# Tree attention on one core: all work in groups of eight heads, stores of eight heads after the loads, V copies shared out anew, the first K and Q in fp32

## The chip, the cores and the metric

The kernel runs on one core of one Trainium2 chip. The metric is the device time of one execution in microseconds (us); lower is better. Times of the kernel before come from three runs; the profile is of one further execution.

## The reference

Attention over 96 independent heads (8 x 12) of 512 positions with 64 values each. A query may look at itself and at its ancestors in a binary tree whose node i has the parent (i - 1) // 2, so at ten keys at most. Inputs and output are fp32.

```
scores = np.einsum('bhqd,bhkd->bhqk', Q, K) * scale
scores = scores + (1 - mask) * (-1e9)
weights = np.exp(scores - np.max(scores, axis=-1, keepdims=True))
weights = weights / (np.sum(weights, axis=-1, keepdims=True) + 1e-10)
return np.einsum('bhqk,bhkd->bhqd', weights, V).astype(np.float32)
```

## The kernel before

**Work.** The 96 heads are taken two at a time: 48 pairs, and one pass of the main loop for each. A partition p holds the four nodes 4p to 4p+3 of a head. For pair i TensorE (PE) transposes K and Q into the PSUM tile `kqp` (L233), VectorE (DVE) copies that to the bf16 tile `kq` (`evac`, L259), PE makes the scores in two PSUM tiles (`scores1`, L270 and L275, and `scores2`, L293 and L299; the mask is a product of code vectors added to the scores), ScalarE (ACT) takes the exponentials (L281, L304), PE multiplies with V (`values`, L328) into the PSUM tile `ob`, and DVE divides by the row sums (`norm`, L351 and L352) into the output tile `of`. The PSUM pools for scores, transposes and products have one buffer each.

**V has to be laid out anew.** Loaded V (`vst`) is copied into one of two tiles `vt` of sixteen heads each, with the column of ones already in it. Three helpers do it, all recorded at L198: `spread_top` copies 32 partitions to one of four places (four copies), `spread_l7` copies two slots of 32 partitions (four copies), and `spread_leaves` two slots of 64 partitions (two copies). Before the change a group of V is sixteen heads. DVE makes nearly all of top and l7 and one of the two leaf copies, ACT makes the other leaf copies, and GpSimd (POOL) makes only the top copies of heads 0 to 7.

**Loads and stores.** K, Q and V are cast from fp32 to bf16 by the DMA, and all of these loads are issued by POOL (`load`, L185). K and Q tiles hold eight heads, in four buffers each; V tiles hold sixteen, in three. A store (`store`, L360) writes four heads, 512 KB, from one of 14 tiles `of`; POOL issues 23 of them, SP and ACT the last four heads. Everything POOL does lies in one list, `pool_program`, and after each pass `pool(i)` issues from its head as long as the next entry is `ready`. Loads and stores alternate in it from the load of heads 48 on. The main loop of a pass is: scores1(i), scores2(i), values(i-1), norm(i-1), transpose(i+2) and evac(i+2), spread(i), pool(i).

**Waits that the code does not name.** The framework adds a semaphore wait wherever an instruction depends on another engine's. The DMAs of POOL use eight semaphores in turn, so a DMA of POOL also waits until the DMA eight places before it in POOL's list has landed. POOL works its list in order: what stands behind a waiting entry waits too.

**At the start** the constants come by two queues: `ptile` (permutations) by SP, `ctile` (mask codes) by ACT; then POOL loads K and Q of two heads, V of four heads, and so on. PE runs products of zeros (`fill`) meanwhile.

Of the kernel before, what the change touches and what calls it, by code (L numbers as in the profile page):

```python
# [98 lines left out]
def kernel(  # L99
# [13 lines left out]
    NQ = NH // 4  # L113
    NP = 2 * NQ
    KB, VB = 8, 16
    assert NH % VB == 0
# [19 lines left out]
    vloads = ctx.enter_context(tc.tile_pool(name="vloads", bufs=3))  # L136
# [3 lines left out]
    opool = ctx.enter_context(tc.tile_pool(name="opool", bufs=14))  # L140
# [3 lines left out]

    ptile = consts.tile([P, perm_np.shape[1]], bf16)
    nc.sync.dma_start(out=ptile[:, :], in_=perm_dram.ap())
    ctile = consts.tile([P, code_np.shape[1]], bf16)
    nc.scalar.dma_start(out=ctile[0:BITS, :], in_=code_dram.ap())
# [21 lines left out]
    for n in range(NV):  # L170
        vt_n = consts.tile([P, VB, 5, D + 2], bf16, name=f"vt{n}")
        nc.vector.memset(vt_n[:, :, :, D:D + 1], 1.0)
        vts.append(vt_n)

    nc.vector.tensor_copy(out=ctile[64:64 + BITS, :], in_=ctile[0:BITS, :])
# [4 lines left out]
    def load(kept, pool, name, size, src, h0, n):  # L180

        b = h0 // size
        if h0 % size == 0:
            kept[b] = pool.tile([P, size, 4, D], bf16, name=name)
        nc.gpsimd.dma_start(  # L185
            out=kept[b][:, h0 % size:h0 % size + n, :, :].rearrange("p h t d -> p h (t d)"),
            in_=src[:, h0:h0 + n, :],
        )

    def load_qk(h0, n):  # L190
        load(ksts, loads, "kst", KB, Kr, h0, n)
        load(qsts, loads, "qst", KB, Qr, h0, n)

    def load_v(h0, n):
        load(vsts, vloads, "vst", VB, Vr, h0, n)

    def copy(eng, out, in_):
        (eng.copy if eng is nc.scalar else eng.tensor_copy)(out=out, in_=in_)  # L198

    def spread_top(eng, j, o, h0, h1):  # L200
        copy(
            eng, vts[o % NV][32 * j:32 * j + 32, h0:h1, 0, 0:D],
            vsts[o][0:32, h0:h1, UNITS[TOP + j][1], :],
        )

    def spread_leaves(eng, r, o, h0, h1):

        p = 64 if r else 0
        copy(
            eng, vts[o % NV][p:p + 64, h0:h1, 1 + r:4 + r:2, 0:D],  # L210
            vsts[o][64:128, h0:h1, r:3 + r:2, :],
        )

    def spread_l7(eng, quad, o, h0, h1):

        first, slot, step = ((2, 0, 3), (2, 2, -1), (1, 3, -3), (1, 1, 1))[quad]
        src = vsts[o][32:64, h0:h1, slot, :]
        src = bass.AP(
            src.tensor, src.offset, [list(src.ap[0]), list(src.ap[1]), [step * D, 2], [1, D]]
        )  # L220
        copy(eng, vts[o % NV][32 * quad:32 * quad + 32, h0:h1, first:first + 3:2, 0:D], src)

    def transpose_one(dst, i, a, t, units, st, perm):

        step = units[1] - units[0]
        if units[2] - units[1] == step:
            dst = dst[64 * a:64 * a + 64, units[0]:units[3] + 1:step, :]
        else:
            gap = units[2] - units[0]
            dst = dst[64 * a:64 * a + 64, units[0]:units[0] + 2 * gap, :].rearrange(  # L230
                "p (x y) c -> p x y c", x=2
            )[:, :, 0:2, :]
        nc.tensor.transpose(  # L233
            out=dst, in_=st[2 * i // KB][:, 2 * i % KB + a, t, :], identity=perm
        )
# [84 lines left out]
    def values(i):  # L320

        if i not in obs:
            obs[i] = psO.tile([P, 2, 512], fp32, name="ob")
        ob = obs[i]
        e1, e2, vt = ets[i], e2s[i % NE], vts[(2 * i // VB) % NV]

        def product(e, a, t, tile_v, lo=0, hi=128, **flags):
# [3 lines left out]
                rhs=vt[:, 2 * i % VB + a, tile_v, 0:D + 1],  # L331
# [3 lines left out]
        for a in range(2):  # L335
# [4 lines left out]
        for a in range(2):  # L340
# [4 lines left out]
    def norm(i):  # L345
        q, r = divmod(i, 2)
        if r == 0:
            ofs[q] = opool.tile([P, 4, 4, D], fp32, name="of")
        o4 = obs[i][:, :, 0:260].rearrange("p a (t c) -> p a t c", c=D + 1)
        rec = small.tile([P, 2, 4, 1], fp32, name="rec")  # L350
        nc.vector.reciprocal(out=rec[:, :, :, :], in_=o4[:, :, :, D:D + 1])  # L351
        nc.vector.tensor_tensor(  # L352
            out=ofs[q][:, 2 * r:2 * r + 2, :, :],
            in0=o4[:, :, :, 0:D],
            in1=rec[:, :, :, :].to_broadcast([P, 2, 4, D]),
            op=ALU.mult,
        )

    def store(eng, q, h0=0, n=4):
        eng.dma_start(  # L360
            out=Or[:, 4 * q + h0:4 * q + h0 + n, :],
            in_=ofs[q][:, h0:h0 + n, :, :].rearrange("p h t d -> p h (t d)"),
        )


    def pool_program():

        def tops(h0, h1):
            return [(spread_top, nc.gpsimd, j, 0, h0, h1) for j in range(4)]

        def stores(*qs):
            return [(store, nc.gpsimd, q) for q in qs]

        ops = [(load_qk, 0, 2), (load_v, 0, 4), (load_qk, 2, 2), (load_qk, 4, 4), (load_v, 4, 4)]
        ops += [(load_v, 8, 8), (load_qk, 8, 4)] + tops(0, 4) + [(load_qk, 12, 4)] + tops(4, 8)
        ops += [(load_qk, 16, 8), (load_v, 16, 8), (load_v, 24, 8), (load_qk, 24, 8)]
        ops += [(load_v, 32, 8), (load_v, 40, 8), (load_qk, 32, 8)]
        ops += [(load_v, 48, 8), (load_v, 56, 8), (load_qk, 40, 8)]
        for g, qs in ((6, (0,)), (7, (1,)), (8, (2, 3)), (9, (4, 5))):
            ops += [(load_v, 8 * g + 16, 8), (load_qk, 8 * g, 8)] + stores(*qs)  # L380
        ops += [(load_qk, 80, 4)] + stores(6, 7) + [(load_qk, 84, 4)] + stores(8, 9)
        ops += [(load_qk, 88, 4)] + stores(10, 11, 12) + [(load_qk, 92, 2)] + stores(13, 14)
        ops += [(load_qk, 94, 2)] + stores(*range(15, NQ - 1))
        return ops

    def ready(op, i):

        f, args = op[0], op[1:]
        if f is load_qk:
            return i >= 4 * (args[0] // KB) - 15  # L390
        if f is load_v:
            return i >= (-1, -1, -1, 3, 11, 15)[args[0] // VB]
        if f is spread_top:
            return True
        return 2 * i >= 4 * (args[1] + 1)

    def early(i):

        v, s = nc.vector, nc.scalar
        l7 = lambda ks, o, h0, h1: [(spread_l7, v, k, o, h0, h1) for k in ks]  # L400
        top = lambda ks, o, h0, h1: [(spread_top, v, k, o, h0, h1) for k in ks]
        leaf = lambda ks, o, h0, h1: [(spread_leaves, s, k, o, h0, h1) for k in ks]
        if i == 0:
            return l7(range(4), 0, 0, 4) + leaf((0, 1), 0, 0, 4)
        if i == 1:
            return l7(range(4), 0, 4, 8) + leaf((0, 1), 0, 4, 8)
        if i == 2:
            return top(range(4), 0, 8, 16)
        if i == 3:
            return l7(range(4), 0, 8, 16) + leaf((0, 1), 0, 8, 16)  # L410
        if i in (6, 7, 8):
            h = (0, 8)
        elif i in (9, 10, 11):
            h = (8, 16)
        else:
            return []
        n = i % 3
        return [top(range(3), 1, *h) + leaf((0,), 1, *h),
                top((3,), 1, *h) + l7((0, 1), 1, *h) + leaf((1,), 1, *h),
                l7((2, 3), 1, *h)][n]  # L420

    def spread(i):

        if i < 12:
            todo = early(i)
        else:
            v, s = nc.vector, nc.scalar
            o, k = divmod(i + 7, 8)
            if o < 2 or o >= NH // VB:
                todo = []  # L430
            else:
                top = [(spread_top, v, j) for j in range(4)]
                l7 = [(spread_l7, v, j) for j in range(4)]
                leaf = [(spread_leaves, v, 0)] + [(spread_leaves, s, 1, h, h + 8) for h in (0, 8)]
                todo = [top[:2], top[2:], leaf[:2], l7[:1], l7[1:2] + leaf[2:], l7[2:3], l7[3:], []]
                if o == 2:
                    todo = [[], [], [], top[:3], top[3:] + leaf[:2], l7[:2] + leaf[2:], l7[2:], []]
                todo = [op[:3] + (o,) + (op[3:] or (0, VB)) for op in todo[k]]
        for op in todo:
            op[0](*op[1:])  # L440

    program = pool_program()

    def pool(i):
        while program and ready(program[0], i):
            op = program.pop(0)
            op[0](*op[1:])

    AHEAD = {1: (2,), 2: (3,), 3: (4, 5)}

    pool(-1)
    fill(0, 9)
# [4 lines left out]
    fill(0, 8)  # L457
    transpose(1)
    fill(0, 4)
# [4 lines left out]
    for i in range(1, NP + 1):  # L464
# [3 lines left out]
        if i >= 2:  # L468
            values(i - 1)
            norm(i - 1)  # L470
# [6 lines left out]
        if i == NP - 1:  # L477
            store(nc.sync, NQ - 1, 0, 2)
    assert not program
    store(nc.sync, NQ - 1, 2, 1)  # L480
    store(nc.scalar, NQ - 1, 3, 1)

# [29 lines left out]
```

## Time and profile before

| | |
|---|---|
| median of three runs | 138.98 us (138.44 to 139.29) |
| the profiled execution: time, span | 139.43 us, 136.6 us |
| busy: PE, DVE, ACT, POOL | 115.4, 108.1, 100.9, 62.7 us |
| read from and written to HBM | 38.01 MB, 12.58 MB |
| DMA issues by POOL | 72, between 1.27 and 129.3 us |
| mean granted TensorE clock | 0.974 |

The span is what the profile shows; 2.8 us of the execution's time lie outside it. A row of groups reads: line, engine, operation, written tile and read tile, partitions x elements, count, then busy time, mean ns of one, and the idle time of the engine before it with its releaser. A timeline row reads: start, duration, engine, line, operation. For a load the GB/s of the profile count the bytes that land, and a cast load lands half of what it reads.

### The profile page before, as it was taken

What the parts mean: (1) busy time and instruction counts of PE and PEld (TensorE: products, weight loads), DVE (VectorE), ACT (ScalarE), POOL (GpSimd) and SP (SyncE); (2) the same over time, 40 slices, a digit from 0 to 9 for tenths busy, and PEclk for the clock granted to TensorE, in tenths of its full rate; (3) what the DMA queues carried; (4) which work ended last, traced back from release to release, by engine and by line L of the source; (5) the groups of instructions that cost most, each with busy time, mean ns of one, the idle gap of its engine ahead of it and who ended that gap; (6) DMA issues with size and microseconds to landing.
All of it is one profiled execution on the core that took longest, in us unless ns stands there. A gap on an engine that the chain in (4) does not pass through costs nothing.

```text
span 136.6 us, 5453 instructions
## 1 busy us (share of the span) xinstructions
PE 115.4 (85%) x2420; PEld 79.6 (58%) x2421; DVE 108.1 (79%) x220; ACT 100.9 (74%) x116; POOL 62.7 (46%) x84
## 2 busy tenths in 40 slices
PE   6999867795998968779999999999998999879820
PEld 2345545573675646557676766666765667657510
DVE  3344997869879999989999899999899988665440
ACT  4083977659799898568997879996879977785900
POOL 6997987323420362342262253342446746644200
PEclk9999999999599999999999999999999999999995
DMA  3999999999999999999999999999999999999972
GB/s 88 143 156 193 197 196 201 194 200 196 197 198 198 198 199 199 197 198 197 276 201 200 279 198 225 326 204 212 333 299 278 330 281 359 337 354 404 354 303 91
DMA packets 41737, 32.06 MB, mean 235 GB/s; under 512 B 1226, under 2 KB 38730, under 8 KB 41714
## 3 DMA queue, kind: packets, MB, share of 16 engines
q0 software_dynamic: 40960, 30.94, 125.1%
q1 hardware_dynamic: 560, 0.56, 1.2%
q8 instruction: 18, 0.29, 0.8%
q10 hardware_dynamic: 194, 0.23, 0.6%
q14 instruction: 5, 0.04, 0.1%
HBM read 38.01 MB, written 12.58 MB: 370 GB/s over the span
## 4 chain that ended last, share of the span: by engine, by line
DMA 56%; PE 23%; POOL 6%; ACT 6%; issue 4%; DVE 1%; POOLq 0%; ACTq 0%
DMA vst<-in_V_dram 44%; DMA out_dram<-of 11%; PE ob L328 8%; PE kqp L233 5%; PE s L270 3%; PE s L293 3%; POOL kst L185 2%; ACT e L304 2%; POOL qst L185 2%; PE s L299 2%; PE s L275 2%; ACT e L281 2%; ACT vt L198 2%; POOL vt L198 1%; DVE of L352 1%
## 5 line engine op out<-in xcount | busy, mean ns | idle before, releaser
L281 ACT ACTIVATE e<-s 128x1024 bf16<-128x1024 f32 x48 | 49.1, 1024 | 25.8 <-PE s L275 25.2
L328 PE MATMUL ob<-vt,e 128*128 128x65 bf16 (+1 forms) x960 | 38.6, 198 | 6.9 <-DVE of L352 6.0
L328 PEld LDWEIGHTS <-e 128*128 128x128 bf16 (+1 forms) x960 | 30.5, 103 | 15.2 <-DVE of L352 6.5
L304 ACT ACTIVATE e<-s 128x768 bf16<-128x768 f32 x48 | 38.6, 804 | 0.0
L198 DVE COPY vt<-vst 32x1024 bf16<-32x1024 bf16 (+3 forms) x68 | 35.1, 516 | 3.2 <-DMA vst<-in_V_dram 1.9
L259 DVE COPY kq<-kqp 128x1024 bf16<-128x1024 bf16 x48 | 32.7, 682 | 4.9 <-PE kqp L233 4.9
L352 DVE TENSOR_TENSOR of<-ob,rec 128x512 f32<-128x512 f32 x48 | 33.2, 692 | 1.7
L360 POOL DMA_DIRECT2D out_dram<-of x23 | 18.3, 797 | 20.1 <-DVE of L352 8.1
L185 POOL DMA_DIRECT2D kst<-in_K_dram x18 | 15.0, 833 | 14.9 <-DMA kst<-in_K_dram 5.5
L270 PE MATMUL s<-ctile 40*128 40x512 bf16 x96 | 19.2, 394 | 2.9 <-ACT e L281 2.6
L233 PE MATMUL kqp<-ptile,kst 128*64 128x128 bf16 x384 | 19.4, 223 | 1.7 <-issue 0.9
L185 POOL DMA_DIRECT2D qst<-in_Q_dram x18 | 15.1, 839 | 12.3 <-PE kqp L233 3.9
L233 PE MATMUL kqp<-ptile,qst 128*64 128x128 bf16 x384 | 19.5, 223 | 0.8 <-DMA qst<-in_Q_dram 0.8
L299 PEld LDWEIGHTS <-kq 64*128 64x128 bf16 x384 | 14.5, 94 | 8.8 <-issue 1.0
L185 POOL DMA_DIRECT2D vst<-in_V_dram x13 | 11.4, 882 | 17.8 <-DVE rec L351 6.6
L275 PE MATMUL s<-kq 64*128 64x512 bf16 x96 | 18.7, 383 | 1.0 <-DVE kq L259 1.0
L351 DVE RECIPROCAL rec<-ob 128x8 f32<-128x8 f32 x48 | 9.9, 205 | 12.1 <-PE ob L328 11.4
L293 PE MATMUL s<-ctile 40*128 40x480 bf16 x96 | 17.9, 368 | 0.8 <-ACT e L304 0.3
L198 ACT COPY vt<-vst 64x1024 bf16<-64x1024 bf16 (+1 forms) x18 | 17.0, 946 | 1.7 <-DMA vst<-in_V_dram 1.4
L299 PE MATMUL s<-kq 64*128 64x64 bf16 (+1 forms) x384 | 17.7, 209 | 0.4 <-issue 0.4
L233 PEld LDWEIGHTS <-kst 128*64 128x64 bf16 x384 | 12.8, 112 | 3.3 <-issue 2.4
L233 PEld LDWEIGHTS <-qst 128*64 128x64 bf16 x384 | 13.9, 113 | 1.2 <-DMA qst<-in_Q_dram 1.0
(17 smaller groups left out, 32.8 us busy)
## 6 DMA issues: line engine op xcount, KB each, us to landing
out_dram<-of POOLq DMA_DIRECT2D x23, 512.0 KB, 9.8
vst<-in_V_dram POOLq DMA_DIRECT2D x11, 512.0 KB, 19.0
kst<-in_K_dram POOLq DMA_DIRECT2D x8, 512.0 KB, 18.4
qst<-in_Q_dram POOLq DMA_DIRECT2D x8, 512.0 KB, 19.2
kst<-in_K_dram POOLq DMA_DIRECT2D x6, 256.0 KB, 10.4
qst<-in_Q_dram POOLq DMA_DIRECT2D x6, 256.0 KB, 10.4
kst<-in_K_dram POOLq DMA_DIRECT2D x4, 128.0 KB, 7.5
qst<-in_Q_dram POOLq DMA_DIRECT2D x4, 128.0 KB, 7.1
```

The costliest lines, as they stand in the source:

```text
L185: nc.gpsimd.dma_start(out=kept[b][:, h0 % size:h0 % size + n, :, :].rearrange("p h t d -> p h (t d)"), in_=src[:, h0:h0 + n, :],)
L198: (eng.copy if eng is nc.scalar else eng.tensor_copy)(out=out, in_=in_)
L233: nc.tensor.transpose(out=dst, in_=st[2 * i // KB][:, 2 * i % KB + a, t, :], identity=perm)
L259: nc.vector.tensor_copy(out=kq[:, :, :, :].rearrange("p k (x y) c -> p k x y c", y=2), in_=src)
L270: nc.tensor.matmul(out=sp[:, a, :], lhsT=k1code[64 * a:64 * a + BITS, :], rhs=q1code[64 * a:64 * a + BITS, :], start=True, stop=False,)
L275: nc.tensor.matmul(out=sp[:, a, :], lhsT=keys(i, a, TOP), rhs=qTs[i][64 * a:64 * a + 64, :, :].rearrange("p t c -> p (t c)"), start=False, ...
L281: nc.scalar.activation(out=et[:, :, :, :].rearrange("p a t c -> p (a t c)"), in_=sp[:, :, :].rearrange("p a c -> p (a c)"), func=AF.Exp, s ...
L293: nc.tensor.matmul(out=flat[:, a, 32:512], lhsT=k2code[64 * a:64 * a + BITS, :], rhs=q2code[64 * a:64 * a + BITS, 32:512], start=True, sto ...
L299: nc.tensor.matmul(out=flat[:, a, lo:hi], lhsT=keys(i, a, TILE2[t]), rhs=qTs[i][64 * a:64 * a + 64, :, :].rearrange("p t c -> p (t c)")[:, ...
L304: nc.scalar.activation(out=e2s[i % NE][:, :, :, 32:128].rearrange("p a t c -> p (a t) c"), in_=sp[:, :, :, 32:128].rearrange("p a t c -> p ...
L328: nc.tensor.matmul(out=ob[lo:hi, a, 65 * t:65 * t + 65], lhsT=e[:, a, PLACE[t], lo:hi], rhs=vt[:, 2 * i % VB + a, tile_v, 0:D + 1], **flags,)
L352: nc.vector.tensor_tensor(out=ofs[q][:, 2 * r:2 * r + 2, :, :], in0=o4[:, :, :, 0:D], in1=rec[:, :, :, :].to_broadcast([P, 2, 4, D]), op=A ...
```

## The change

All pools and helpers go by groups of eight heads. In detail:

- K and Q of heads 0 and 1 come in fp32 by SP and ACT, ahead of the constants (both constants now by SP), and DVE and ACT cast them (`first_pair`). POOL starts with V of four heads.
- Output tiles hold eight heads; there are twelve, one for each group, so none is used twice. A store writes eight heads. Stores begin at pass 33, one in a pass, after the last load has been issued in pass 32. All stores are issued by POOL. The last group gets 4 heads at pass 46 and two stores of 2 heads after the loop.
- From pass 12 on, pass i makes for the next group one l7 copy on DVE, and on POOL either two top copies or one leaf copy; ACT copies only for groups 0 to 3. `after` makes POOL's first copy of a pass wait for DVE's.
- The last pair's products go to the transposes' PSUM bank, head by head, and it is normalised in two halves. Transposes of pair 3 come one pass earlier.

The order of POOL's instructions in the built kernel has 61 DMAs (46 loads, 15 stores) and 69 copies, where it had 72 DMAs and 8 copies; DVE has 60 copies of V instead of 68, ACT 11 instead of 18.

```diff
-    KB, VB = 8, 16
+    GB = 8
+    NG = NH // GB
...
-    vloads = ctx.enter_context(tc.tile_pool(name="vloads", bufs=3))
+    vloads = ctx.enter_context(tc.tile_pool(name="vloads", bufs=4))
...
-    opool = ctx.enter_context(tc.tile_pool(name="opool", bufs=14))
+    opool = ctx.enter_context(tc.tile_pool(name="opool", bufs=NG))
...
+    for name, eng, src in (("k", nc.sync, Kr), ("q", nc.scalar, Qr)):
+        first[name] = consts.tile([P, 2, 4, D], fp32, name=f"first_{name}")
+        eng.dma_start(
+            out=first[name][:, :, :, :].rearrange("p h t d -> p h (t d)"), in_=src[:, 0:2, :]
+        )
...
-    nc.scalar.dma_start(out=ctile[0:BITS, :], in_=code_dram.ap())
+    nc.sync.dma_start(out=ctile[0:BITS, :], in_=code_dram.ap())
...
+    def first_pair():
+        nc.vector.tensor_copy(out=ksts[0][:, 0:2, :, :], in_=first["k"][:, :, :, :])
+        nc.scalar.copy(out=qsts[0][:, 0:2, :, :], in_=first["q"][:, :, :, :])
+        nc.vector.tensor_copy(out=ctile[64:64 + BITS, :], in_=ctile[0:BITS, :])
...
-        if i not in obs:
+        if i == NP - 1:
+            obs[i] = psT.tile([P, 2, 512], fp32, name="kqp")
+        elif i not in obs:
             obs[i] = psO.tile([P, 2, 512], fp32, name="ob")
...
+    def store(g, h0=0, n=GB):
+        nc.gpsimd.dma_start(
+            out=Or[:, GB * g + h0:GB * g + h0 + n, :],
+            in_=ofs[g][:, h0:h0 + n, :, :].rearrange("p h t d -> p h (t d)"),
+        )
...
+        every = range(4)
+        return {
+            0: l7(0, every, 0, 4) + [(spread_top, DVE, j, 0, 0, 4) for j in every]
+            + leaf(ACT, 0, (0, 1), 0, 4),
+            1: l7(0, every, 4, 8) + top(0, every, 4, 8) + leaf(ACT, 0, (0, 1), 4, 8),
+            3: l7(1, every, 0, 4) + top(1, every, 0, 4) + leaf(ACT, 1, (0, 1), 0, 4),
+            5: l7(1, every, 4, 8) + top(1, every, 4, 8) + leaf(ACT, 1, (0, 1), 4, 8),
+            6: l7(2, (0,)) + top(2, (0, 1)) + leaf(ACT, 2, (0,)),
+            7: l7(2, (1, 2)) + top(2, (2, 3)) + leaf(ACT, 2, (1,)),
+            8: l7(2, (3,)),
+            9: l7(3, (0,)) + top(3, (0, 1)),
+            10: l7(3, (1, 2)) + top(3, (2, 3)) + leaf(ACT, 3, (1,)),
+            11: l7(3, (3,)) + leaf(POOL, 3, (0,)),
+        }.get(i, [])
+
+    def spread(i):
+
+        g, j = i // 4 + 1, i % 4
+        if i < 12:
+            todo = early_copies(i)
+        elif g < NG:
+            todo = [(spread_l7, DVE, j, g)]
+            if j < 2:
+                todo += [(spread_top, POOL, k, g) for k in (2 * j, 2 * j + 1)]
+            else:
+                todo += [(spread_leaves, POOL, j - 2, g)]
+        else:
+            todo = []
+        last = None
+        for f, eng, *args in todo:
+            done = f(eng, *args)
+            if eng is DVE:
+                last = done
+            elif eng is POOL and i >= 6 and last is not None:
+                after(done, last)
+                last = None
+
+    def loads_at(i):
+
+        k4 = lambda h: [(load_k, h, 4), (load_q, h, 4)]
+        start = [(load_v, 0, 4), (load_k, 2, 2), (load_q, 2, 2)] + k4(4) + [(load_v, 4, 4)]
+        start += k4(8) + [(load_v, 8, 4)] + k4(12)
+        early = {
+            -1: start, 1: [(load_v, 12, 4), (load_v, 16)],
+            2: [(load_k, 16, 4), (load_q, 16, 4), (load_k, 20, 4)],
+            3: [(load_q, 20, 4), (load_v, 24), (load_k, 24, 4)], 5: [(load_q, 24, 4)],
+            6: [(load_k, 28, 4)], 7: [(load_q, 28, 4), (load_v, 32)],
+            8: [(load_k, 32), (load_q, 32)], 9: [(load_v, 40)], 10: [(load_k, 40)],
+            11: [(load_q, 40), (load_v, 48)], 12: [(load_k, 48), (load_q, 48)],
+        }
+        if i in early:
+            return early[i]
+        g, j = i // 4 + 3, i % 4
+        if i < 13:
             return []
+        if j == 0:
+            return [(load_q, GB * g)] if g < NG else []
+        if j < 3 and g + 1 < NG:
+            return [((load_v, load_k)[j - 1], GB * (g + 1))]
+        return []
+
+    stored = []
+
     def pool(i):
-        while program and ready(program[0], i):
-            op = program.pop(0)
-            op[0](*op[1:])
+        for f, *args in loads_at(i):
+            f(*args)
+        if i >= 33:
+            for g in range(len(stored), (i - 4) // 4 + 1):
+                if len(stored) < i - 32:
+                    stored.append(g)
+                    store(g)
...
-    AHEAD = {1: (2,), 2: (3,), 3: (4, 5)}
+    AHEAD = {1: (2, 3), 2: (), 3: (4, 5)}
...
-            norm(i - 1)
+            norm(i - 1, ((0, 1), (1, 2)) if i == NP else ((0, 2),))
...
-        if i == NP - 1:
-            store(nc.sync, NQ - 1, 0, 2)
-    assert not program
-    store(nc.sync, NQ - 1, 2, 1)
-    store(nc.scalar, NQ - 1, 3, 1)
+        if i == NP - 2:
+            store(NG - 1, 0, 4)
+    store(NG - 1, 4, 2)
+    store(NG - 1, 6, 2)
```

The loop runs to pass 48 (`range(1, NP + 1)`), as before.

## The prediction, made before the changed kernel ran

> **What bounds the kernel now.** I read the page first: span, the slices of DMA and the traffic with HBM.
>
> ```profile
> span 136.6 us, 5453 instructions
> ...
> DMA  3999999999999999999999999999999999999972
> GB/s 88 143 156 193 197 196 201 194 200 196 197 198 198 198 199 199 197 198 197 276 201 200 279 198 225 326 204 212 333 299 278 330 281 359 337 354 404 354 303 91
> ...
> HBM read 38.01 MB, written 12.58 MB: 370 GB/s over the span
> ```
>
> From the third slice to the last but one the DMA engines are busy, so the question is whether they also move bytes at their best. For that I read two stretches, one with loads alone and one with stores alone (columns as in the page; last the GB/s):
>
> ```profile
> 20.00:60.00 40.00, 32.67 (x714) 23.28 (x716) 35.07 (x71) 31.92 (x36) 14.31 (x16) 0.96 1.46 198
> ...
> 124.00:128.00 4.00, 3.89 (x86) 2.71 (x81) 2.38 (x6) 3.45 (x4) 0.80 (x2) 1.00 1.03 399
> ```
>
> Casting loads land 198 GB/s for 40 us without a dip; stores run at 399, in the best slice 404. A load of eight heads lands 512 KB, so it takes 524/198 = 2.65 us; a store of eight heads is 1 MB, 1049/404 = 2.6 us. All traffic: 36 x 2.65 = 95.3 us and 12 x 2.6 = 31.2 us, 126.5 us of the span of 136.6. Only 10.1 us are not DMA at full rate: the first slices (88, 143 and 156 instead of 198: some 3.7 us by slices of 3.4 us), the last ones, and the end. The DMA engines bound this kernel, and no order of copies can make it much shorter than 130.
>
> POOL's own rows show how loads are paced:
>
> ```profile
> 31.31 0.88 POOL L185 DMA_DIRECT2D vst<-in_V_dram  x1 [1.35 <-DMA vst<-in_V_dram]
> 33.73 0.88 POOL L185 DMA_DIRECT2D vst<-in_V_dram  x1 [1.54 <-DMA vst<-in_V_dram]
> 36.61 1.08 POOL L185 DMA_DIRECT2D kst<-in_K_dram  x1 [2.00 <-DMA kst<-in_K_dram]
> ```
>
> One issue in about 2.65 us, each after a wait for a landing: the one eight places before it. Some 8 MB are on their way, 18 to 19 us from issue to landing, so POOL may be several us late without the DMA running dry.
>
> The compute engines come close behind. Groups kept apart by shape:
>
> ```profile
> L352 DVE TENSOR_TENSOR of<-ob,rec 128x512 f32<-128x512 f32 x48 | 33.2, 692 | 1.7
> L259 DVE COPY kq<-kqp 128x1024 bf16<-128x1024 bf16 x48 | 32.7, 682 | 4.9 <-PE kqp L233 4.9
> L351 DVE RECIPROCAL rec<-ob 128x8 f32<-128x8 f32 x48 | 9.9, 205 | 12.1 <-PE ob L328 11.4
> L198 DVE COPY vt<-vst 32x1024 bf16<-32x1024 bf16 x28 | 13.8, 491 | 0.5
> ...
> L198 POOL COPY vt<-vst 32x256 bf16<-32x256 bf16 x8 | 3.2, 399 | 1.3 <-DMA vst<-in_V_dram 1.0
> ```
>
> The tail, from the last rows of the timeline and the DMA answer for the last 11.6 us:
>
> ```profile
> 130.40 2.24 SPq L360 DMA_DIRECT2D out_dram<-of  x2
> ...
> 131.58 0.69 DVE L352 TENSOR_TENSOR of<-ob,rec 128x512 f32<-128x512 f32 x1
> 132.30 0.40 ACTq L360 DMA_DIRECT2D out_dram<-of  x1
> ```
> ```profile
> out_dram<-of POOLq DMA_DIRECT2D x1, 512.0 KB, 5.8
> out_dram<-of SPq DMA_DIRECT2D x1, 256.0 KB, 4.6
> out_dram<-of SPq DMA_DIRECT2D x1, 128.0 KB, 3.2
> out_dram<-of ACTq DMA_DIRECT2D x1, 128.0 KB, 3.3
> ```
>
> The last store is issued at 132.30, lands 3.3 us later at 135.6, and 1.0 us ends the span.
>
> **The change, part by part.**
>
> *Start.* Nothing of the traffic goes away, but K and Q of the first pair are issued at about 0.74 (when SP and ACT issue now) instead of 1.27, and POOL's first issue carries four heads instead of two. That is 4 of 288 loaded heads (95.3 x 4/288 = 1.3 us of DMA) plus half a load of four (0.65 us) earlier: of the 3.7 us lost now I take 2 back. The start also costs DVE and ACT a cast each (at most the 0.64 us of the mask codes' copy) and four top copies on DVE (0.35 us each, 1.4 us); pair 1 needs its data from DMAs of POOL that land later than that, so this is hidden.
>
> *Loads.* The same bytes at the same rate, now with no store between them. Pass 12 needs V of heads 32 to 39. They are the last of 100 heads in order of issue, landed at about 2 + 95.3 x 100/288 = 35 us; with the copies, pass 12 is at 36 to 39 us (now 44.31).
>
> *Steady passes.* DVE per pair: 692 + 682 + 205 + one l7 copy 491 = 2.07 us. PE per pair by the chain of waits: 2.11 us (scores to scores, 93.06 to 95.18). ACT: 1024 + 804 = 1.83 us. POOL per group of four pairs: three loads at 0.88, four top copies of 512 elements, two leaf copies of 1024. The only POOL copies in the trace have 256 elements and take 0.40 us. Bounds: in proportion, 0.8 and 1.6 us; or with half of the 0.40 fixed, 0.6 and 1.0 us. Sum 7.0 to 9.0 us, or 1.76 to 2.26 us a pair, later 0.2 more for the stores. I take 8.2, nearer the upper end, as the DVE works beside it. Now the last 23 pairs take 74.80 to 128.04 by ACT's rows, 2.31 us each, with more copies on ACT and DVE. With 2.31 us the remaining 36 pairs take 83 us from 38, and the last normalisation ends near 38 + 83 + 2 = 123 us: before the stores have left the queue. So what this part wins or loses up to 6 us is hidden behind the DMA.
>
> How far DVE and POOL hinder each other matters here: DVE's copies at L198 last 271 ns at the least and 917 at the most.
> The Trainium skill (SBUF — State Buffer, "SBUF: two separate sides") says that a two-port copy of DVE and a GpSimd instruction exclude each other for the whole instruction; it speaks against moving copies to POOL. By it an l7 copy could wait out a leaf copy, and as an estimate from that page's rule the pace would come to 2.07 + 1.0 to 1.6 us in a pass with a leaf copy, and the time to the slow-pace case below. The row (917 at most, 491 in the mean, beside 0.88 us issues of POOL) agrees that there is a delay, not that it is the rule in each pass.
>
> *Stores.* Eleven stores of eight heads are issued from pass 33 on, some 2.3 us apart, each 2.6 us of DMA, behind loads that are all issued by then. So the queue stays full. Until the store of the last group's first four heads (pass 46) has landed: 95.3 + 11.5 x 2.6 = 125.2, with 3 us for start and ramp and 0.8 for the landing: **129.0 us**.
>
> *The end.* Here lies the cost. The loop runs to pass 48, where `(i - 4) // 4 + 1` is 12, and eleven groups are stored. So pass 48 stores group 11 whole, though its heads 0 to 3 are stored in pass 46 and 4 to 7 after the loop. POOL's last DMAs in the built order are stores of 8, 4, 8, 2 and 2 heads, the last four all from one tile. They write the same part of the output, so each waits for what it overlaps: the second of eight for the landing of the four, the two of two for the landing of the eight. What could run in the queue at once becomes three round trips:
> - four heads landed, then eight heads issued: the smallest POOL load lands in 3.4 us at the least, 0.65 of it transfer, so 2.75 + 2.6 = 5.4 us; upper bound by the 512 KB store above, 5.8 + 1.3 = 7.1. Nothing else is on the queue, so 5.5.
> - two issues of two heads, 0.75 us apart; the last lands 3.4 (POOL's least) to 4.6 us (SP's 256 KB) after its issue: 4.15 to 5.35, I take 4.2.
> - to the end of the span 1.0.
> Together 10.7 us. The halved last normalisation and the other PSUM bank shorten the compute tail by at most half of 692 + 205 = 0.45 us, hidden by the queue.
>
> *Sum.* 129.0 + 10.7 = 139.7 us of span, 3.1 more than now, plus the 2.8 outside it: 142.5 against this execution's 139.43. The median of the runs lies 0.45 below it, so **142.1 us**.
>
> **Rivals.**
> 1. *The passes are the bound, not the queue.* If DVE and POOL wait on each other, or POOL (9.0 us and stores a group) sets the pace, the last normalisation comes after 129. That needs (129 - 40)/36 = 2.47 us a pair. Against it: 2.31 now with more work on DVE. For it: from pair 1 to 47 the mean now is (128.04 - 12.74)/46 = 2.51, and POOL has little slack. With 2.6: 38 + 93.6 + 2 = 133.6, and the same round trips behind it: 144.3 of span, 146.7 us.
> 2. *Not slower: the queue drains sooner.* Stores of eight heads have 8 KB in a row in each partition instead of 4. If that made them a tenth faster, 29.9 us would be 27 and the time 139; it decides when the four heads land before 126 us, which needs some 400 GB/s of HBM traffic from the second us on. Against it: the 198 GB/s (396 read) is flat for 40 us, and stores have not passed 404.
> 3. *The change doesn't do what the order says*: the second store of group 11 costs nothing, because nothing waits on it. Then the two small stores follow in the queue: 129 + 2 x 0.65 + 1.0 = 131.3, so 133.7 us. Against it: the overlap of the writes is in the code.
>
> **How the numbers follow.** Forecast 62%, range 140.2 to 144.8 (the landing at 129 from 127.5, all of the start won, to 130; the round trips from 10.5 to 11.9). Rival 1 26%, 144 to 149. Rival 2 8%, 138 to 140. Rival 3 4%. For 8 in 10: 140.0 to 147.0, which leaves out rival 3, most of rival 2 and the upper part of rival 1. A measurement of this kernel tells about 1% from no change, 137.6 to 140.4. Faster: rival 3 and a little of rival 2, 0.05. Same: most of rival 2 and the forecast's lowest edge, 0.09. Slower: 0.86.
>
> **What would show it.** 13.6 MB written instead of 12.58. In the last 11 us POOL issues a store of eight heads after a wait for a landing, then two of two heads after another, while PE, DVE and ACT are idle and GB/s falls. GB/s of 198 until about 97 us, then near 400. The first 3.4 us above 88 GB/s. DVE L198 copies of 32x1024 near 500 ns; POOL copies of 32x512 between 600 and 800 ns. The forecast is wrong if GB/s dips between 20 and 125 us (POOL too late), if the last normalisation comes after 129, or if the last stores don't wait.

## The result, and the profile after

The changed kernel takes 148.63 us (median of four runs, 147.54 to 150.2), the kernel before 138.97. A run in a slower state, with a longer time and mostly a lower granted clock (here the 150.2), counts in the median but not in the ratio, here and below. The ratio is 1.067, with a 95% interval of 1.059 to 1.075: slower by 6.7%. Slower was forecast, but by 2.2%, and 148.63 lies above the range of 140 to 147. The profiled execution took 149.07 us with a span of 147.3.

The page after, with the rows that answer to those shown first of before (slices of 3.68 us):

```profile
span 147.3 us, 5481 instructions
...
DMA  4999999998799999999999999999999999995243
GB/s 125 223 194 199 193 197 197 197 188 106 98 191 198 199 197 199 197 198 202 194 199 197 198 201 194 199 197 206 341 399 402 404 397 405 399 394 215 110 176 142
...
HBM read 38.01 MB, written 13.63 MB: 351 GB/s over the span
```

Read three places. The HBM row has 1.05 MB more written: group 11 is stored twice, as the order of instructions said. The GB/s fall to 106 and 98 at about 33 to 41 us: the queue ran nearly dry, which was not forecast. And in the last four slices, some 15 us, PE, DVE and ACT do next to nothing and the GB/s are 110 to 215 instead of 400.

The chain that ended last, in order of time (start, duration, what):

```profile
127.30 0.76 DMA out_dram<-of
128.06 9.40 issue
137.46 0.01 POOLq L385
137.47 4.86 DMA out_dram<-of
142.33 0.28 issue
142.62 0.71 POOL out_dram L385
143.32 0.71 POOLq L539
```

The store of the last group's first four heads is issued at 127.30. What the chain calls "issue" for 9.40 us is POOL waiting: the next store, of the whole group, overlaps that one and starts only at 137.47. The stores of two heads start at 142.62, after that one landed. The DMA answer from 120 us to the end (slices of 0.68 us; last column us from issue to landing) gives the landings:

```profile
DMA  9999999999999999998774310002999500098100
GB/s 396 384 414 396 402 414 378 420 396 390 402 402 396 408 414 396 414 372 330 306 294 180 132 66 0 0 0 84 408 432 402 210 0 0 0 384 336 48 0 0
...
out_dram<-of POOLq DMA_DIRECT2D x1, 512.0 KB, 9.6
out_dram<-of POOLq DMA_DIRECT2D x2, 256.0 KB, 2.5
```

127.30 + 9.6 = 136.9 us for the four heads. The last normalisation had ended at 130.7, so the compute engines stood still for 16.6 us. Its last row:

```profile
130.27 0.42 DVE L377 TENSOR_TENSOR of<-kqp,rec 128x256 f32<-128x256 f32 x1
```

Where the dip comes from shows in POOL's timeline and in four windows:

```profile
23.73 0.74 POOL L189 DMA_DIRECT2D qst<-in_Q_dram  x1
30.79 1.25 POOL L209 COPY vt<-vst 32x512 bf16<-32x512 bf16 x2 [6.31 <-DVE vt L209]
31.99 0.74 POOL L189 DMA_DIRECT2D kst<-in_K_dram  x1
```
```profile
25.00:30.00 5.00, 4.55 (x110) 3.29 (x104) 4.24 (x11) 4.96 (x7) 0.00 (x0) 1.00 1.46 197
30.00:35.00 5.00, 4.37 (x99) 3.06 (x94) 4.63 (x11) 4.90 (x7) 3.41 (x6) 1.00 1.28 171
35.00:40.00 5.00, 5.00 (x118) 3.67 (x116) 4.02 (x8) 4.20 (x5) 4.58 (x7) 1.00 0.69 85
40.00:45.00 5.00, 4.60 (x110) 3.30 (x106) 4.79 (x10) 4.27 (x6) 3.89 (x6) 1.00 1.37 183
```

POOL issued a load at 23.73, and its next instruction, a copy of pass 6, waited 6.31 us for DVE's copy of the same pass. Five loads of passes 6 to 8 stood behind it, and one more copy that waits. What was on its way lasted to about 33 us (the lowest window of 1 us, from 38 to 39, has 28 GB/s); against 198 GB/s the three windows from 30 to 45 lack 27, 113 and 15, times 5 us: 3.9 us of the queue's work. The granted TensorE clock was 0.67 from 20 to 25 us, so a part of the 6.31 us may be slower passes; but the run with the loads in front (below) has 0.66 in the same window and no dip.

### The profile page after: what moved, and what is told of

It is laid out like the page before. It is cut to its first block, busy times and chain, and to the rows that moved or that the text cites. A ratio compares the mean times of both kernels' runs of the same rounds, so it can differ in the third digit from the quotient of the medians.

```text
span 147.3 us, 5481 instructions
## 1 busy us (share of the span) xinstructions
PE 114.8 (78%) x2413; PEld 80.7 (55%) x2413; DVE 103.0 (70%) x215; ACT 92.6 (63%) x110; POOL 96.2 (65%) x134
## 5 line engine op out<-in xcount | busy, mean ns | idle before, releaser
L209 POOL COPY vt<-vst 32x512 bf16<-32x512 bf16 (+2 forms) x69 | 46.5, 674 | 28.6 <-DVE vt L209 22.7
L347 PEld LDWEIGHTS <-e 128*128 128x128 bf16 (+1 forms) x960 | 31.0, 103 | 10.4 <-issue 2.1
L377 DVE TENSOR_TENSOR of<-ob,rec 128x512 f32<-128x512 f32 x47 | 32.5, 692 | 1.6
L209 DVE COPY vt<-vst 32x1024 bf16<-32x1024 bf16 (+2 forms) x60 | 28.4, 473 | 1.6
L385 POOL DMA_DIRECT2D out_dram<-of x15 | 12.8, 857 | 18.1 <-issue 9.4
L250 PE MATMUL kqp<-ptile,kst 128*64 128x128 bf16 x384 | 20.0, 225 | 4.2 <-DVE kq L276 2.0
L250 PEld LDWEIGHTS <-kst 128*64 128x64 bf16 x384 | 13.5, 113 | 5.9 <-issue 5.0
L189 POOL DMA_DIRECT2D kst<-in_K_dram x16 | 13.3, 834 | 0.0
L189 POOL DMA_DIRECT2D qst<-in_Q_dram x16 | 13.3, 832 | 0.0
L189 POOL DMA_DIRECT2D vst<-in_V_dram x14 | 12.2, 874 | 0.9 <-POOLq L528 0.8
```

The source lines that it names most:

```text
L189: nc.gpsimd.dma_start(out=kept[g][:, h0 % GB:h0 % GB + n, :, :].rearrange("p h t d -> p h (t d)"), in_=src[:, h0:h0 + n, :],)
L209: return (eng.copy if eng is nc.scalar else eng.tensor_copy)(out=out, in_=in_)
L250: nc.tensor.transpose(out=dst, in_=st[2 * i // GB][:, 2 * i % GB + a, t, :], identity=perm)
L347: nc.tensor.matmul(out=ob[lo:hi, a, 65 * t:65 * t + 65], lhsT=e[:, a, PLACE[t], lo:hi], rhs=vt[:, 2 * i % GB + a, tile_v, 0:D + 1], **flags,)
L377: nc.vector.tensor_tensor(out=ofs[g][:, 2 * r + a0:2 * r + a1, :, :], in0=o4[:, :, :, 0:D], in1=rec[:, :, :, :].to_broadcast([P, a1 - a0, ...
```

## The experiments

Theory A: the time is the queue's. The store of four heads lands at 136.9 because all loads and stores are in front of it, with the stall of pass 6 inside; then three round trips follow because group 11 is stored twice. Rivals: the second store costs only its bytes (B), the passes set the end (C), the turns of DVE and POOL protect more than they cost (D). The kernel before ran beside every group of runs, with medians of 138.82 to 139.08 us, so medians may be compared; the ratio is always to the kernel before.

**The second store left out.**

```diff
-        if i >= 33:
+        if 33 <= i < NP:
```

> The second store of group 11 in pass 48 is left out, all else as after; the output stays whole. Theory A (three round trips behind a queue that drains at 136.9 us): the two stores of two heads follow in the queue, issued at about 131 and 132 us, and land with or just behind the stores of eight; the span is 137 to 138.5 us, the time 139 to 141, 8 to 9.5 us less than after. Rival B (the second store costs only its 1 MB of traffic): 2.6 us less, 146. HBM writes 12.58 MB.

Measured: 141.54 us, ratio 1.020 (1.013 to 1.026), span 139.3. So 7.1 us less than after, not 2.6: B is out. It is a little above A's 139 to 141. POOL's last rows, and the landings after 118 us:

```profile
127.26 0.77 POOL L385 DMA_DIRECT2D out_dram<-of  x1 [4.35 <-DVE of L377]
129.31 0.72 POOL L385 DMA_DIRECT2D out_dram<-of  x1 [1.28 <-DVE of L377]
130.95 0.72 POOL L385 DMA_DIRECT2D out_dram<-of  x1 [0.92 <-DVE of L377]
```
```profile
out_dram<-of POOLq DMA_DIRECT2D x1, 512.0 KB, 9.3
out_dram<-of POOLq DMA_DIRECT2D x2, 256.0 KB, 7.4
```

The three last stores now wait only for DVE. The last one, issued at 130.95, lands 6.9 us later (7.4 is the mean of the two), at 137.9, where a store of 256 KB with nothing before it took 2.5. The queue still ends the kernel.

**The loads in front of POOL's copies.**

```diff
-            3: [(load_q, 20, 4), (load_v, 24), (load_k, 24, 4)], 5: [(load_q, 24, 4)],
-            6: [(load_k, 28, 4)], 7: [(load_q, 28, 4), (load_v, 32)],
-            8: [(load_k, 32), (load_q, 32)], 9: [(load_v, 40)], 10: [(load_k, 40)],
+            3: [(load_q, 20, 4), (load_v, 24), (load_k, 24, 4)],
+            5: [(load_q, 24, 4), (load_k, 28, 4), (load_q, 28, 4), (load_v, 32), (load_k, 32)],
+            7: [(load_q, 32)], 9: [(load_v, 40)], 10: [(load_k, 40)],
```

> The loads of K and Q of heads 28 to 31, V of 32 to 39 and K of 32 to 39, which stood behind POOL's copies of passes 6 to 8, are issued in pass 5; the second store stays. Theory A (the queue ran dry because POOL waited 6.3 us for DVE's copy of pass 6, and the queue sets the end): no dip of GB/s between 30 and 42 us, the loads end 3.9 us sooner, the store of four heads lands at about 133, the time is 144 to 145.5. Rival C (the passes set the end, with the last normalisation at 130.7): the dip goes, but the store of four heads lands less than 1 us sooner, and the time stays within 1 us of 148.6.

Measured: 145.92 us, ratio 1.051 (1.044 to 1.059), span 143.5. Its POOL rows:

```profile
27.06 0.88 POOL L189 DMA_DIRECT2D vst<-in_V_dram  x1 [0.39 <-ACT e L321]
28.45 0.96 POOL L189 DMA_DIRECT2D kst<-in_K_dram  x1 [0.51 <-PE ob L347]
31.00 1.25 POOL L209 COPY vt<-vst 32x512 bf16<-32x512 bf16 x2 [1.59 <-DVE vt L209]
...
125.22 0.76 POOL L385 DMA_DIRECT2D out_dram<-of  x1 [4.08 <-DVE of L377]
133.71 0.90 POOL L385 DMA_DIRECT2D out_dram<-of  x1 [7.72 <-issue]
```

POOL's copy of pass 6 starts no sooner (31.00 after 30.79), but nothing is behind it that the queue needs, and its GB/s stay at 198 from 12 to 96 us. The store of four heads lands at 125.22 + 8.0 = 133.2 (136.9 after):

```profile
out_dram<-of POOLq DMA_DIRECT2D x1, 512.0 KB, 8.0
```

The store of eight heads moves from 137.47 to 133.71, 3.8 us: the dip's cost in these two executions. C forecast less than 1.

**No turns.** The dependency of POOL's copies on DVE's is not made.

```diff
-            elif eng is POOL and i >= 6 and last is not None:
+            elif eng is POOL and i >= 99 and last is not None:
```

> The extra dependency of POOL's first copy of a pass on DVE's copy is left out; POOL's copies then wait for V alone. The second store stays. Theory A: POOL's copies of pass 6 start when V of heads 16 to 23 has landed (about 24.5 us instead of 30.8), the loads behind them are issued some 5 us sooner, the dip is gone and the time is 144 to 146, as with the loads ahead. Rival D (the turns protect DVE): DVE's copies of 32x1024 rise from 532 ns to 700 or more, the passes slow from 2.42 to 2.6 us and the last normalisation moves to 136 or later: 148 to 153.

Measured: 145.10 us, ratio 1.045 (1.040 to 1.049). POOL's rows, and DVE's group:

```profile
24.79 1.25 POOL L209 COPY vt<-vst 32x512 bf16<-32x512 bf16 x2
25.99 0.74 POOL L189 DMA_DIRECT2D kst<-in_K_dram  x1
```
```profile
L209 DVE COPY vt<-vst 32x1024 bf16<-32x1024 bf16 x40 | 24.5, 612 | 1.2
```

POOL's copies of pass 6 start 6.0 us sooner, and the loads with them: the dip is gone and the time close to that of the run before, so the added dependency was what made the queue run dry. D's slowing is there (612 ns after 532) but small: 40 x 80 ns, off the path, as the last normalisation ends at 129.8 and the store of four heads lands at 133.7.

**Both mends: no second store, loads in front.**

> No second store, and the loads ahead as in the run before. Theory A: the queue drains at about 133, the last normalisation stays near 130, the small stores follow in the queue: span 134 to 135.5, time 136.5 to 138.5, 10 to 12 us less than after and faster than before. Rival C (the passes set the end): last normalisation at 130.7, then issue, landing and end, 0.8 + 3.4 + 1.0: span 136, time 138.5 to 139, no better than without the second store alone.

Measured: 138.11 us, ratio 0.996 (0.993 to 1.000), span 135.6. The two costs roughly add: 7.1 and 2.7 one by one, 10.5 together. Without them the change brings the kernel back to where it was, and hardly beyond. As stated by A (136.5 to 138.5), though C's 138.5 is too near to be told apart by the time alone. Hence the next ones, all on top of this kernel.

**Both mends without turns.** The edit is that of the run without turns.

> No second store, loads ahead, and POOL's copies no longer made to wait for DVE's. Theory A (the wait did harm only by what stood behind POOL's copies, and that is mended already): the same as with both mends, 137.6 to 138.6. Rival D (copies side by side slow DVE; its copies of 32x1024 took 612 ns without turns and 551 with them): the passes slow by up to 0.06 us each, the last normalisation comes 2 us later, 139 to 140.5.

Measured: 137.69 us, ratio 0.992 (0.990 to 0.994). As A says, once the loads are in front, the turns neither help nor harm the time. The last store of this kernel, and then of the one with both mends:

```profile
127.14 0.72 POOL L385 DMA_DIRECT2D out_dram<-of  x1 [0.92 <-DVE of L377]
```
```profile
130.29 0.72 POOL L385 DMA_DIRECT2D out_dram<-of  x1 [1.08 <-DVE of L377]
```

It is issued 3.15 us sooner here, since the passes end sooner, but lands 7.6 us after its issue instead of 3.9: at 134.7 instead of 134.2. So the passes do not set the end, the queue does; this is what parts A from C, better than the time with both mends did. The kernel is faster than the one before by 0.8%, with an interval of 0.6 to 1.0%; but the spans are 135.8 to 136.2 against 136.0 to 136.6, some 0.3 us, and the rest of the 1.1 us lies outside the span, unexplained.

**The first pair by POOL again.**

```diff
-        nc.vector.tensor_copy(out=ksts[0][:, 0:2, :, :], in_=first["k"][:, :, :, :])
-        nc.scalar.copy(out=qsts[0][:, 0:2, :, :], in_=first["q"][:, :, :, :])
...
-        start = [(load_v, 0, 4), (load_k, 2, 2), (load_q, 2, 2)] + k4(4) + [(load_v, 4, 4)]
+        start = [(load_k, 0, 2), (load_q, 0, 2), (load_v, 0, 4), (load_k, 2, 2), (load_q, 2, 2)]
+        start += k4(4) + [(load_v, 4, 4)]
```

> As with both mends, but the first pair's K and Q come by POOL in bf16 as in the kernel before (K, Q, then V of four heads), the codes come by ACT, and the two casts are gone. Theory A (the queue sets the end, and by 12 us the start had moved 0.5 MB more than in the kernel before): 1.0 to 1.5 us slower, 139.1 to 139.6. Rival E (the start brings nothing, as the first exponential starts at 7.3 us where it was 7.4): within 0.4 us of 138.1.

Measured: 139.91 us, ratio 1.006 (1.002 to 1.009), 1.8 us slower than with both mends. The windows of 4 us at the start, first this kernel, then the one with both mends:

```profile
4.00:8.00 4.00, 3.27 (x34) 1.38 (x33) 0.69 (x1) 0.74 (x1) 4.00 (x6) 1.00 1.17 145
8.00:12.00 4.00, 2.36 (x42) 1.42 (x40) 3.68 (x9) 2.22 (x4) 3.18 (x5) 1.00 1.33 173
```
```profile
4.00:8.00 4.00, 3.50 (x34) 1.77 (x33) 2.57 (x6) 1.28 (x2) 3.88 (x6) 1.00 1.32 195
8.00:12.00 4.00, 3.37 (x59) 2.06 (x58) 3.44 (x9) 2.70 (x5) 1.64 (x3) 1.00 1.44 194
```

E is out, and 139.91 lies a little above A's 139.1 to 139.6. The first exponential starts at 7.3 us in both: no earlier pass 0. The queue is full sooner with the new start, and the store of four heads lands at 132.8 instead of 134.8. But pass 1 is earlier too (first exponential at 11.59 instead of 12.63), and the granted TensorE clock was 0.56 and 0.50 in this kernel's windows from 12 to 20 us (1.00 in the other). Its last normalisation ends at 133.1 instead of 130.0, and then comes the last store:

```profile
133.40 0.72 POOL L377 DMA_DIRECT2D out_dram<-of  x1 [2.75 <-DVE of L369]
```

It lands 2.7 us after its issue, much like a store with nothing before it (2.5). So in this execution the passes set the end, and how the 1.8 us divide among the queue, the passes and the clock is not shown.

**Fewer stores.** Groups 0 to 3 are not stored, so a third of the output is missing.

```diff
-                    store(g)
+                    if g >= 4:
+                        store(g)
```

> As with both mends, but groups 0 to 3 are not stored, so a third of the output is missing: 4.2 MB or 10.5 us of the queue's work. Theory A in its strong form (the queue alone sets the end): about 8 to 10 us less, 128 to 130. Rival C (the passes stand close behind it): the last normalisation stays at 130, then issue, landing and end, 0.7 + 3 + 1: span 134.5, 136.5 to 137.5, 1 to 1.5 us less.

Measured: 132.55 us, ratio 0.951 (0.945 to 0.958): 5.6 us less by the medians, 6.1 by the three runs in the ratio (median 132.05), between A's strong form (8 to 10) and C (1 to 1.5). Neither holds as stated. Its GB/s (slices of 3.28 us) say why:

```profile
GB/s 89 254 187 196 197 196 198 197 197 198 195 198 198 198 200 198 201 195 200 196 198 197 199 197 199 198 198 197 198 202 122 9 214 390 375 398 368 402 365 69
```

The queue ran empty at 102 us, since the first store that is left stands in pass 37. So some of what was taken out came back as idle queue: against 198, 198 and 400 GB/s the slices with 122, 9 and 214 lack 1.3, 3.1 and 1.5 us, 5.9 together. That is more than the 4.4 to 4.9 us that are missing from 10.5, so the idle queue alone accounts for them. The last normalisation ended at 125.5 here, and the last store, issued at 125.83, landed 4.1 us later, so the queue was not empty then. With both mends the queue is the bound, but the passes come close behind: there the last store lands 3.9 us after its issue, only 1.4 more than the 2.5 of a store with nothing before it.

**No copies on POOL from pass 12 on.** The output of those heads is computed with stale V.

```diff
+            if eng is POOL and i >= 12:
+                continue
```

> As with both mends, but POOL's copies of V from pass 12 on are left out, so that half of the heads from 32 on are computed with stale V. Theory A: DVE's copies fall from 556 ns towards 420, the passes from 2.4 us to 2.3 or less, the last normalisation from 130 to 126 or less; the queue still drains at 133 to 134, so the time stays within 0.7 us of 138.1. Rival F (POOL's late issues cost the queue something all along): the loads end before 101 us instead of 102.3 and the time falls by more than 1 us.

Measured: 137.77 us, ratio 0.992 (0.991 to 0.994): 0.3 us less, as A says. Two of A's details missed: DVE's copies fall to 486 ns, not towards 420, and the last normalisation ends at 128.5, not 126. Yet 48 copies less on POOL are worth hardly anything. DVE's copies, this kernel and then the one with both mends:

```profile
L209 DVE COPY vt<-vst 32x1024 bf16<-32x1024 bf16 x40 | 19.5, 486 | 1.2
```
```profile
L209 DVE COPY vt<-vst 32x1024 bf16<-32x1024 bf16 x40 | 22.3, 556 | 1.2
```

**Stores of four heads.**

```diff
-                    store(g)
+                    store(g, 0, 4)
+                    store(g, 4, 4)
```

> As with both mends, but each store of eight heads in the loop is issued as two of four heads, as long as those of the kernel before. Theory A (the size of a store changes neither the rate nor the order of the queue): store phase near 400 GB/s as with eight heads, time within 0.5 us of 138.1. Rival 2 of the prediction (eight heads in one store move faster): store phase below 390 GB/s and 1 to 3 us slower. The other way, if the uneven drain of the last 4 us comes from long stores: last landing 1 us or more sooner, 137 or less.

Measured: 138.32 us, ratio 0.996 (0.993 to 0.999); 399 GB/s from 104 to 128 us, 398 with stores of eight. Between four and eight heads the size of a store makes no difference that shows: rival 2 of the prediction is out, and nothing here puts the slow drain of the last microseconds down to the long stores.

**V of the first four heads in fp32 too**, by ACT's queue, on top of both mends without turns; the copies of these heads cast.

```diff
+    first["v"] = consts.tile([P, 4, 4, D], fp32, name="first_v")
+    nc.scalar.dma_start(
+        out=first["v"][:, :, :, :].rearrange("p h t d -> p h (t d)"), in_=Vr[:, 0:4, :]
+    )
...
-        start = [(load_v, 0, 4), (load_k, 2, 2), (load_q, 2, 2)] + k4(4) + [(load_v, 4, 4)]
+        start = [(load_k, 2, 2), (load_q, 2, 2)] + k4(4) + [(load_v, 4, 4)]
```

> As with both mends and without turns, and V of heads 0 to 3 comes in fp32 by ACT as well, its copies casting from there, so that POOL's first load is K of heads 2 and 3. Theory A (the queue sets the end, and before 5 us it is not full): another 0.5 MB of reads leave POOL's list and run while the queue is still filling, 0.5 to 1.3 us less, 136.4 to 137.2. Rival C (the passes set the end): copies that cast from fp32 are no faster, pass 1 starts no sooner, and the time stays within 0.4 us of 137.7.

Measured: 137.82 us, ratio 0.990 (0.984 to 0.995); the three runs in the ratio go from 137.18 to 138.28, the fourth is 140.07. Not settled: the interval covers that of the kernel without this edit (0.990 to 0.994), so neither A's 0.5 to 1.3 us nor C's nothing is shown. No version is shown to beat 137.7.

## Why the prediction was wrong, point by point

- **The bound, the second store and its three round trips: right.** From the landing of four heads to the end of the span it forecast 10.7 us and got 147.3 - 136.9 = 10.4. The store of eight heads took 142.62 - 137.47 = 5.15 (forecast 5.5), the rest 4.7 (5.2), and 0.6 passed before the first issue (forecast 0). That the sum is so close is partly luck: the small stores landed in 2.5 us (forecast 3.4 to 4.6), and 1.5 us followed (forecast 1.0). Leaving the store out brought 7.1 us.
- **"So the queue stays full" is the step that failed.** The prediction allowed POOL to be "several us late" with 8 MB on the way. Its own sign of being wrong, a dip of GB/s between 20 and 125 us, came true at 33 to 41 us. Later on, from 45 us, the queue did stay full. Before the stall POOL had issued loads of 84 heads, many of them of four heads, half as long. At 95.3/288 us a head they are 27.8 us of work, gone at about 32 us from a start near 4. The prediction didn't count what stands behind a waiting POOL copy in that phase. The added wait of pass 6 was 6.31 us; it cost 3.8 us by the shift of the store of eight heads, 2.7 by the medians with the loads in front and 3.5 without turns. Without the stall the kernel takes 145.1 to 145.9 us, inside the range, so the stall is what carried it out.
- **129.0 us for the landing of four heads was also too low without the stall:** 125.22 + 8.0 = 133.2 with the loads in front, 4.2 more. Three pieces can be read off. The 198 GB/s count other traffic too (the page has 0.31 MB of instruction loads, queue q8): in the run with the loads in front POOL's queue itself moved 16.37 MB in the 84 us from 12 to 96, which is 195 GB/s and makes all loads 1.5 us longer. The queue doesn't end at once: in the seven slices of 0.68 us from 372 to 66 GB/s, shown above, the busy share falls from 9 to 1 tenths, and what they lack to 400 is 1.9 us, where 0.8 was allowed. The start loses 3.6 us of the first 8, not 3 (145 and 205 GB/s in two windows of 4 us, 1.40 MB; without 0.26 of constants, and with 0.52 of fp32, that is 0.62/0.198 + 1.3 = 4.4 us of work). That is 3.2 of the 4.2 us. In the same run that queue stored 7.94 MB from 104 to 124 us, 397 GB/s, where the sum took 404: 0.5 us more. About 0.5 us remains unplaced.
- **The start: sized 2 us, measured 1.8** by undoing it. The number fits, but the mechanism (a queue that is full sooner) is not shown by it, as the passes set the end of that run and its clock was lower.
- **POOL's copies: inside the bounds, at the lower end.** The profile after:

```profile
L209 POOL COPY vt<-vst 32x512 bf16<-32x512 bf16 x40 | 24.2, 604 | 18.4 <-DVE vt L209 16.6 <-PE ob L347 0.6
L209 POOL COPY vt<-vst 64x1024 bf16<-64x1024 bf16 x17 | 17.6, 1035 | 6.9 <-DVE vt L209 6.1 <-PE ob L347 0.6
L209 POOL COPY vt<-vst 32x256 bf16<-32x256 bf16 x12 | 4.7, 393 | 3.3 <-DMA vst<-in_V_dram 2.9
```

- **The pace of the passes: too fast a forecast, but hidden as said.** ACT's row of pass 12 starts at 42.00 us (36 to 39 forecast) and that of pass 47 at 126.79: 2.42 us a pass, not 2.31, and the last normalisation ends at 130.7, not 123. That is after 129, the second sign of being wrong that the prediction had named, and the pace is close to the 2.47 of rival 1. But it is still 6 us before the four heads land, and in the run without second store and turns the end stayed where it was with passes that ended 3 us sooner. So rival 1 is not what happened, though its 144 to 149 us cover the measured time.
- **Rivals 2 and 3** are out: stores of four and eight heads run alike, and the second store was waited for.
- **Outside the span** lie 1.8 us of the profiled execution, 2.8 before; why, is not known.
- **Two slips in the working.** By its own terms the likely range is 138.0 to 141.9 us of span, 140.4 to 144.3 us of time, not 140.2 to 144.8. And the 917 ns of a DVE copy, held against a mean of 491, belong to a copy of 2048 elements (mean of that shape 712), the 491 to those of 1024.

Summed: 142.1 + 3.7 (stall, 136.9 - 133.2) + 4.2 (landing without it) - 0.3 (round trips) - 1.0 (outside the span) = 148.7. This is bookkeeping from single executions; shown by edits are the stall and the second store, while the pieces of the 4.2 are read off traces.

On the locked port: the Trainium skill (SBUF — State Buffer, "SBUF: two separate sides") says a DVE copy that uses the shared port pair and a GpSimd instruction block each other for a whole instruction. Here DVE's copies of 32x1024 took 486 ns in the mean with no POOL copies from pass 12 on, 532 to 587 with turns and 573 to 613 without. The longest single DVE copy took 785 ns after and 1200 in the first run without turns, where about half of those of 32x1024 still took some 420. That fits a block that is met now and then, though no run here isolates it; a wait of a whole POOL copy in each pass, which the prediction priced as the worst case, did not come.

## What to carry to other kernels

When the DMA queue is the bound, a wait added to the engine that issues the loads is priced by what stands behind it in that engine's list and by how many bytes are on their way at that moment, in the start phase too, not only in the steady one. Put the loads in front of the copies that wait. And look in the built order for transfers that overlap in the memory they write: two writes of the same rows become round trips at the end, where nothing covers them. Here the second of them took 5.15 us for 1 MB, and leaving it out brought 7.1 us, where its bytes alone would have been 2.6.

## What the hardware showed that was not expected

- A GpSimd copy of bf16 costs about 0.18 us and 0.84 ns an element of its row: 393, 604 and 1035 ns for 256 and 512 elements on 32 partitions and 1024 on 64. Beside it DVE copies 1024 elements on 32 partitions in 486 to 613 ns in the mean.
- The chain's label "issue" stood for a wait on a DMA's landing (9.40 us); only the landing column showed it.
- A full queue of stores does not end at once: after, the mean busy share of the 16 DMA engines falls from 9 tenths to 1 over some 4.5 us; stores of four heads instead of eight did not make the kernel end sooner.
